# The opening of a decoder layer: norm factors loaded as rows, the first norm in another order, and idle turns on TensorE

## The chip, the core and the metric

The kernel runs on one core of one Trainium2 chip. The metric is the device time of one execution in microseconds (us); lower is better. The core's engines run in parallel, each through a queue of its own: TensorE (PE in the profile; its weight loads are PEld), VectorE (DVE), ScalarE (ACT), GpSimd (POOL) and SyncE (SP), which only issues transfers (DMAs). ACT and POOL issue DMAs too. "SPq" in a view is an instruction of SP's queue. An engine works through its queue in order and waits at an instruction until the semaphores that it names are reached. PE writes to PSUM banks; everything else lives in SBUF (128 partitions).

## What is computed

One layer of a decoder: 16 learned meta tokens are put before 1024 tokens of width 1024, then come a half-step SwiGLU block, a mixer (HGRN2 recurrence beside stick-breaking attention), and a second half-step SwiGLU block, all in float32:

```
def rms_norm(x, gain):
    y = xf * lax.rsqrt(jnp.mean(xf * xf, axis=-1, keepdims=True) + RMS_EPS)
    return (y * gain)

def swiglu(h, w_in, w_out):
    g, u = jnp.split(h @ w_in, 2, axis=-1)
    return (jax.nn.silu(g) * u) @ w_out

h = h + 0.5 * swiglu(rms_norm(h, ffn1_norm), ffn1_w_in, ffn1_w_out)
u = rms_norm(h, mix_norm) @ w_in
...
h = h + o @ w_out
h = h + 0.5 * swiglu(rms_norm(h, ffn2_norm), ffn2_w_in, ffn2_w_out)
```

The part at stake is the first line that uses `ffn1_norm`: the norm of x and the start of its product with `ffn1_w_in`.

## The kernel before

**Precision and tiling.** Each float32 operand is split into a rounded high part (by ACT) and a remainder (by DVE), and each product is three matmuls: high by high, low by high, high by low. A product of 128 output columns with a K of 512 is thus 4 x 3 = 12 matmuls of 128x512, all from one line (L459, `times`). The FFN products use a seven-product scheme (Strassen-Winograd) over 2x2 blocks of x and of the weights; the x operands are called B11, B21, T2, T3, T1, T4 and B22. B11 is the norm's columns 0 to 511 of the first 512 tokens, B21 columns 512 to 1023 of the same tokens.

**The opening.** x comes as eight blocks of 128 tokens by 1024 columns (`ra`, four, then `rb`, four), issued by SP (L820). For each block the squares of a row are summed (`row_sum`: ACT L773 or DVE L770), ACT takes the root of the mean plus epsilon (L778) and DVE the inverse (L779), and DVE scales the block in place (`row_scale`, L785). PE turns 128x128 pieces with the identity into PSUM (`turned`, L794, tile `xps`; one bank per k, that is per 128 columns of x, with a quarter for each block). Then for each k ACT makes the high part times the gain of that k (`first`, L844), and DVE the low part (L845). The gains stand as a column per k, tile `g1`; `ng1` is its negative, needed later.

**Order.** In the opening the queues of PE, ACT, DVE and SP follow the program's order exactly (`manual_schedule`). PE's order is written by hand up to the end; the other engines' queues outside the opening, and POOL's, are put in order by a planner that estimates times and takes what is ready first. The first eight products of weights (four pairs of gate and up, called `quad`) are generators: each call of `next(order[i])` does one step. For a quad the first two steps load half a weight block each (L379 is the load and its rounding), the third multiplies by B11 (12 matmuls into a bank of tag `qa`) and ACT copies the bank (L483), the fourth adds B21. `order[0]` and `order[2]` are the first quad, `order[1]` and `order[3]` the second. After the lines of the change, a loop goes on through the other steps, two loads ahead, with the work on `rb` hung in between: sums, roots, scalings, turns (`turn_b22`, `turn_b12`, `turn_meta`).

**Before, in the program's order:** sum, root and inverse of blocks 0, 1, 2; their scalings; block 3 alone with a scaling in two halves; load step one of both quads; loads of `rb`; turns of all four blocks for k = 0 to 5 (24); operands k = 0 to 3; load step two of the first quad; operands 4 and 5; first quad by B11 (12 matmuls); turns for k = 6 and 7 (8); operands 6 and 7; second quad by B11.

**Gains.** Ten loads bring the small vectors (`column`, L107): each puts one value on each partition, four bytes a piece. The first (`ffn1_norm`) is issued by ACT at the start, the other nine by SP in `setup_rest` (L113), which is called at the end of the opening. The matrix `ones_d` (all 1/1024) is filled at the start and read much later. POOL's first work is to clear `xm` and `actm` (L1816, L1817), then the identity's diagonal (L80, an `affine_select` over ones from DVE), then the cutting of the masks `sd` and `neg_b` (L129 to L142).

Of the kernel before, what the change touches and what calls it, by code (L numbers as in the profile page):

```python
# [11 lines left out]
F32 = mybir.dt.float32  # L12
# [3 lines left out]
AF = mybir.ActivationFunctionType  # L16
ALU = mybir.AluOpType
# [3 lines left out]
P = 128  # L21
D = 1024
KT = D // P
SEQ = 1024
META = 16
T = META + SEQ
D_FF = 2816
EPS = 1e-6
# [21 lines left out]
class Block:  # L50
# [11 lines left out]
            self.tc.tile_pool(name=name, bufs=bufs, **kw)  # L62
        )

    def column(self, src, n, name):
        t = self.const.tile([P, n], F32, name=name)
        self.loads.append((t, src.rearrange("(k p) -> p k", p=P)))
        return t

    def setup(self):  # L70
        nc, a = self.nc, self.a
        self.loads = []
        self.const = c = self.pool("const")
# [5 lines left out]
        nc.vector.memset(self.ident, 1.0)  # L79
        nc.gpsimd.affine_select(  # L80
            out=self.ident, in_=self.ident, pattern=[[-1, P]],
            compare_op=ALU.is_equal, fill=0.0, base=0, channel_multiplier=1,
        )
# [6 lines left out]
        self.g1 = self.column(a["ffn1_norm"][0], KT, "g1")  # L90
        self.gm = self.column(a["mix_norm"][0], KT, "gm")
        self.g2 = self.column(a["ffn2_norm"][0], KT, "g2")
        self.og = self.column(a["hgrn_out_norm"][0], 4, "og")
        self.l0 = self.column(a["hgrn_lb_logits"][0], 4, "l0")
        self.l1 = self.column(a["hgrn_lb_logits"][1], 4, "l1")
        self.qg, self.kg, self.qg8 = (c.tile([P, 1], F32, name=x) for x in ("qg", "kg", "qg8"))
        for h in range(2):
            s = slice(64 * h, 64 * h + 64)
            self.loads.append((self.qg[s], a["sb_q_norm"].rearrange("a d -> d a")))
            self.loads.append((self.kg[s], a["sb_k_norm"].rearrange("a d -> d a")))  # L100
        self.mx, self.lb, self.lbc = (c.tile([P, 4], F32, name=x) for x in ("mx", "lb", "lbc"))
        self.ident_b, self.neg_b = (c.tile([P, P], BF16, name=x) for x in ("ident_b", "neg_b"))
        self.masks = c.tile([P, len(LEVELS), P], U8, name="masks")
        self.ss = c.tile([P, 9, 2], F32, name="ss_x")
        self.ng1 = c.tile([P, KT], F32, name="ng1")
        self.pick = c.tile([P, 2, META], F32, name="pick")
        nc.scalar.dma_start(*self.loads.pop(0))  # L107

    def setup_rest(self):

        nc = self.nc
        for dst, src in self.loads:
# [651 lines left out]
            eng.dma_start(row[:m], x[r0 - META : r0 - META + m, cols])  # L764

    def row_sum(self, row, i, junk, eng):
        nc, m = self.nc, row.shape[0]
        s = self.ss[:m, i, 0:1]
        if eng is nc.vector:
            return eng.scalar_tensor_tensor(  # L770
                junk[1][:m], row, 1.0, row, ALU.mult, ALU.mult, accum_out=s
            )
        return nc.scalar.activation(junk[0][:m], row, AF.Square, accum_out=s)  # L773

    def row_root(self, row, i):
        m = row.shape[0]
        s, r = self.ss[:m, i, 0:1], self.ss[:m, i, 1:2]
        self.nc.scalar.activation(r, s, AF.Sqrt, bias=self.eps[:m], scale=1.0 / D)  # L778
        self.nc.vector.reciprocal(r, r)  # L779

    def row_scale(self, row, i, parts=1):
        m = row.shape[0]
        for j in range(parts):
            t = row[:, D // parts * j : D // parts * (j + 1)]
            self.nc.vector.tensor_scalar_mul(t, t, self.ss[:m, i, 1:2])  # L785

    def turned(self, rows, ks, banks):

        nc = self.nc
        ps = {k: self.pin.tile([P, 512], F32, tag="q" + x, name="xps", bufs=2)  # L790
              for k, x in zip(ks, banks)}
        for i, row in enumerate(rows):
            for k in ks:
                nc.tensor.transpose(  # L794
                    ps[k][:, i * P : (i + 1) * P], row[:, k * P : (k + 1) * P], self.ident
                )
        return ps

    def open_tokens(self, ops, opened, prepare, rows_at, ev, operands):
# [9 lines left out]
        nc, x = self.nc, self.a["x"][0]  # L809
        stt, sub = nc.vector.scalar_tensor_tensor, nc.vector.tensor_sub  # L810
        g = [self.g1[:, k : k + 1] for k in range(KT)]
        rp = self.pool("rows", ctx=rows_at, side="right")
        junk = [rp.tile([P, D], (BF16, U8)[i], name=f"junk{i}") for i in range(2)]
        order = [q for i in range(0, len(opened), 2) for _ in range(2) for q in opened[i : i + 2]]

        def rows_in(r0):
            got = []
            for i in range(4):
                row = rp.tile([P, D], F32, tag="row", name="row", bufs=8)
                nc.sync.dma_start(row, x[r0 + i * P : r0 + i * P + P])  # L820
                got.append(row)
            return got
# [12 lines left out]
        kept = {}  # L835
# [5 lines left out]
        def first(*ks):  # L841
            for k in ks:
                hi, lo = (t[:, k % 4, :] for t in ops[("B11", "B21")[k // 4]])
                nc.scalar.mul(hi, kept[k], g[k])  # L844
# [17 lines left out]
        first(0, 1, 2, 3)  # L862
# [12 lines left out]
        def turn_b22():  # L875
            kept["b22"] = self.turned(rb, range(4, KT), "bbcc")
# [17 lines left out]
        def turn_meta():  # L894
# [18 lines left out]

        def roots():
            for i, row in enumerate(rb + [meta]):
                self.row_root(row, 4 + i)
            for i in range(2):
                self.row_scale(rb[i], 4 + i)

# [866 lines left out]
    def run(self):  # L1786
        nc, tc, a = self.nc, self.tc, self.a
# [11 lines left out]
        n = 512  # L1799
# [8 lines left out]
        with ExitStack() as c0:  # L1808
            with ExitStack() as c1:
# [6 lines left out]
                nc.gpsimd.memset(self.xm, 0.0)  # L1816
                nc.gpsimd.memset(self.actm, 0.0)  # L1817
                with tc.manual_schedule(engines={nc.tensor.engine}), ExitStack() as c2:
                    ev0 = self.pool("ev10", ctx=c2)
                    self.ahead = self.pool("ahead", ctx=c2)  # L1820
# [89 lines left out]
                    first, hooks, steps_ahead = 32, 54, 58  # L1910
# [20 lines left out]
                with tc.manual_schedule(engines={nc.tensor.engine}), ExitStack() as c2:  # L1931
# [48 lines left out]
                    sums, banks = {}, {}  # L1980
# [426 lines left out]
```

## Time and profile before

| | us |
|---|---|
| median of 3 runs | 1965.85 (1964.18 to 1965.95) |
| profiled execution | 1965.29 |
| its span, first to last instruction | 1963.6 |
| PE busy in the span | 1928.3 |
| before PE's first matmul | 11.43 |

How to read it: the page gives busy time by engine, the chain of work that ended last, and groups of instructions by line. `xps<-ident,row` means that the tile `xps` is written from `ident` and `row`; x24 is a count. In the timeline the first number is the start from the span's beginning, the second the length, and square brackets give how long the engine stood idle before and what it waited for. The times of a matmul record overlap with its neighbours, so a group's length over its count is its rate.

### The profile page before, as it was taken

How to read it: one execution, taken by the hardware profiler on the slowest of the kernel's cores; microseconds unless marked ns; L12 is line 12 of the kernel's file. 1: busy time of each engine (PE TensorE's matmuls, PEld its weight loads, DVE VectorE, ACT ScalarE, POOL GpSimd, SP SyncE). 2: the span in 40 equal slices, each digit the busy share in tenths (PEclk: the TensorE clock that was granted, in tenths of full speed). 3: DMA queues.
4: the chain of work that ended last, by engine and by line, in shares of the span. 5: the costliest groups of instructions: out<-in, count | busy, mean ns of one | idle time of the engine just before them, and what ended most of it. 6: DMA issues, size and time to landing. Idle time of an engine off the chain costs nothing.

```text
span 1963.6 us, 30437 instructions
## 1 busy us (share of the span) xinstructions
PE 1928.3 (98%) x10704; PEld 1622.0 (83%) x10704; DVE 1391.6 (71%) x2186; ACT 851.7 (43%) x1711; POOL 449.8 (23%) x626
## 2 busy tenths in 40 slices
PE   7999999999999999999999999999999999999999
PEld 6888888888888888888888978887888888888887
DVE  6977777877678665567777766667567777767774
ACT  6523343334444544356666635433132332344443
POOL 3010100001000003133333332210544545430000
PEclk9999999999999999999999999999999999999999
DMA  6356787757965415865454167655544444469473
GB/s 211 93 160 174 245 278 237 235 208 280 372 226 185 136 47 144 194 175 148 126 143 126 57 249 216 171 204 181 195 117 140 126 137 119 134 236 330 146 232 113
DMA packets 381688, 355.56 MB, mean 181 GB/s; under 512 B 129040, under 2 KB 284560, under 8 KB 381536
## 3 DMA queue, kind: packets, MB, share of 16 engines
q1 hardware_dynamic: 359728, 288.98, 48.2%
q0 software_dynamic: 20768, 64.63, 9.5%
q8 instruction: 85, 1.39, 0.3%
q14 instruction: 67, 0.55, 0.1%
q10 hardware_dynamic: 1040, 0.00, 0.0%
HBM read 237.95 MB, written 115.57 MB: 180 GB/s over the span
## 4 chain that ended last, share of the span: by engine, by line
PE 91%; DVE 4%; DMA 2%; ACT 2%; issue 1%; POOL 0%; SPq 0%; ACTq 0%; DVEq 0%; POOLq 0%
PE o L741 21%; PE qb L459 18%; PE qc L459 12%; PE qa L459 12%; PE proj L258 5%; PE proj L260 5%; PE proj L259 5%; PE flip L1504 2%; PE wo L259 1%; PE wo L260 1%; PE wo L258 1%; PE mq L1010 1%; PE oacc L1579 1%; PE oacc L1581 1%; PE z L1649 1%
## 5 line engine op out<-in xcount | busy, mean ns | idle before, releaser
L459 PE MATMUL qb<-T,wh 128*128 128x512 f32 x1056 | 344.5, 390 | 1.3 <-ACT T L318 0.8
L459 PEld LDWEIGHTS qb<-T,wh 128*128 128x128 f32 x1056 | 198.1, 188 | 46.1 <-issue 2.5
L459 PE MATMUL qa<-B,wh 128*128 128x512 f32 x696 | 226.8, 391 | 0.0
L258 PE MATMUL proj<-xh,wh 128*128 128x512 f32 (+2 forms) x640 | 213.4, 333 | 2.4 <-ACT st L1151 1.3
L741 PE MATMUL o<-t,w 128*128 128x512 f32 x924 | 211.8, 390 | 0.5 <-DVE u L552 0.5
L260 PE MATMUL proj<-xl,wh 128*128 128x512 f32 (+2 forms) x640 | 209.8, 328 | 0.8 <-DVE xl L1973 0.8
L259 PE MATMUL proj<-xh,wl 128*128 128x512 f32 (+2 forms) x640 | 209.7, 328 | 0.0
L741 PE MATMUL o<-parts 128*128 128x512 f32 x924 | 209.6, 389 | 0.0
L459 PE MATMUL qb<-T,wl 128*128 128x512 f32 x528 | 205.4, 389 | 0.0
L741 PEld LDWEIGHTS o<-t,w 128*128 128x128 f32 x924 | 172.8, 188 | 37.3 <-issue 0.8
L741 PEld LDWEIGHTS o<-parts 128*128 128x128 f32 x924 | 173.4, 188 | 36.0
L371 DVE TENSOR_TENSOR wl<-s,wh 128x512 fp32r<-128x512 f32 x160 | 165.8, 1036 | 50.8 <-ACT wh L369 49.8
L369 ACT CAST wh<-s 128x512 fp32r<-128x512 f32 x160 | 99.7, 624 | 188.5 <-PE qb L459 142.3
L459 PEld LDWEIGHTS qa<-B,wh 128*128 128x128 f32 x696 | 130.6, 188 | 27.3 <-DVE B L845 0.3
L369 ACT CAST wh<-raw 128x512 fp32r<-128x512 f32 x120 | 74.6, 622 | 147.3 <-PE qc L459 99.0
L459 PE MATMUL qa<-B,wl 128*128 128x512 f32 x348 | 135.4, 389 | 0.0
L258 PEld LDWEIGHTS proj<-xh,wh 128*128 128x128 f32 x640 | 120.6, 188 | 14.5 <-ACT st L1151 2.0
L260 PEld LDWEIGHTS proj<-xl,wh 128*128 128x128 f32 x640 | 120.5, 188 | 12.1 <-DVE xl L1973 1.2
L259 PEld LDWEIGHTS proj<-xh,wl 128*128 128x128 f32 x640 | 120.5, 188 | 9.9
L459 PE MATMUL qc<-T,wh 128*128 128x512 f32 x352 | 117.0, 394 | 0.0
L459 PE MATMUL qc<-B,wh 128*128 128x512 f32 x352 | 115.1, 390 | 2.0 <-DVE u L552 1.2
L459 PEld LDWEIGHTS qb<-T,wl 128*128 128x128 f32 x528 | 99.1, 188 | 20.4
(398 smaller groups left out, 3853.9 us busy)
## 6 DMA issues: line engine op xcount, KB each, us to landing
raw<-in_ffn_w_in_dram SPq DMA_DIRECT2D x176, 256.0 KB, 3.9
raw<-in_ffn_w_out_dram SPq DMA_DIRECT2D x112, 256.0 KB, 4.4
w2in<-both SPq DMA_DIRECT2D x28, 512.0 KB, 3.4
raw<-in_w_in_dram SPq DMA_DIRECT2D x25, 512.0 KB, 5.1
ks<-kD SPq DMA_DIRECT2D x32, 260.0 KB, 4.7
wout<-both SPq DMA_DIRECT2D x16, 512.0 KB, 3.8
wh<-w2in SPq DMA_DIRECT2D x27, 256.0 KB, 3.5
wl<-w2in SPq DMA_DIRECT2D x27, 256.0 KB, 3.6
```

The source lines that it names most:

```text
L258: nc.tensor.matmul(ps, wh[:, s], xs, start=k == 0, stop=False)
L259: nc.tensor.matmul(ps, wl[:, s], xs, start=False, stop=False)
L260: nc.tensor.matmul(ps, wh[:, s], xl[:, k, c0 : c0 + n], start=False, stop=k == nk - 1)
L369: nc.scalar.copy(hi, src)
L371: self.block_lo = nc.vector.tensor_sub(lo, src, hi.bitcast(F32))
L459: nc.tensor.matmul(ps, a[:, k, :], b[:, k, :], start=start and k == 0 and i == 0, stop=k == 3 and i == 2, skip_group_check=True,)
L741: nc.tensor.matmul(banks[bank][m], y[:, m * P : (m + 1) * P], z, start=start and at == 0 and e == 0, stop=q == nq - 1 and e == 2, skip_gro ...
L1010: nc.tensor.matmul(ps[at : at + 32, at_g, :], self.xm[:, 4 * h + k, :], got[i, h][:, k, :], start=h == 0 and kk == 0, stop=h == 1 and kk = ...
L1504: self.nc.tensor.transpose(ps[:m, j, :], src[:, s0 : s0 + m], self.ident)
L1579: nc.tensor.matmul(o[:, c], vj, w[0], start=j == 0, stop=False, skip_group_check=True)
L1581: nc.tensor.matmul(o[:64, c], vj[:, :64], w[1], start=False, stop=end, skip_group_check=True)
L1649: nc.tensor.matmul(z, q, ks[0][:, s0 : s0 + n], start=True, stop=False)
```

## The change

The ten small vectors are now loaded as 38 rows of 128 values into `ones_d` by POOL, after the identity's select and the two memsets; PE turns the first eight rows (a 128x8 bank `gps`), DVE copies them to `g1` and makes `ng1`. The other 30 are turned later, after step 10 of the loop (`turn_gains`), and `ones_d` gets its 1/1024 in `setup_rest`. POOL now makes the identity before it clears `xm` and `actm`. PE turns the identity into itself 12 times before the factors' turn, 14 times behind it, and 4 times between blocks 0 and 1 (`idle_turns`). Block 3's squares are summed half on ACT, half on DVE, and the second half's mean goes into the root as its bias. Each block is scaled as soon as its inverse is there; of blocks 2 and 3 only columns 0 to 511 are scaled and turned (k = 0 to 3) before operands 0 to 3, the rest after them. The second quad's products by B11 come right behind the first's, ahead of the turns for k = 4 to 7 of the last two blocks; the loads of `rb` come after the first quad's second weight load.

```
     def setup(self):
-        nc.gpsimd.affine_select(
+        self.ident_at = nc.gpsimd.affine_select(
...
-        nc.vector.memset(self.ones_d, 1.0 / D)
...
-        nc.scalar.dma_start(*self.loads.pop(0))
     def setup_rest(self):
-        for dst, src in self.loads:
-            nc.sync.dma_start(dst, src)
+        nc.vector.memset(self.ones_d, 1.0 / D)
...
+    def gain_rows(self):
+        a, at, got = self.a, 0, []
+        for src in (a["ffn1_norm"][0], a["mix_norm"][0], a["ffn2_norm"][0],
+                    a["hgrn_out_norm"][0], a["hgrn_lb_logits"][0], a["hgrn_lb_logits"][1]):
+            src = src.rearrange("(k p) -> k p", p=P)
+            n = src.shape[0]
+            self.loads.append((self.ones_d[at : at + n, :], src))
+            got.append(self.gains[:, at : at + n])
+            at += n
...
+    def row_root(self, row, i, bias=None):
...
+        self.nc.scalar.activation(
+            r, s, AF.Sqrt, bias=self.eps[:m] if bias is None else bias, scale=1.0 / D
+        )
+        return r
...
+    def turn_row(self, ps, row, i, ks):
+        for k in ks:
+            self.nc.tensor.transpose(
+                ps[k][:, i * P : (i + 1) * P], row[:, k * P : (k + 1) * P], self.ident
+            )
...
         ra = rows_in(0)
         self.masks_blank(sd)
-        for i in range(3):
-            self.row_sum(ra[i], i, junk, nc.vector if i == 1 else nc.scalar)
-            self.row_root(ra[i], i)
-        for i in range(3):
-            self.row_scale(ra[i], i)
-        self.row_sum(ra[3], 3, junk, nc.scalar)
-        self.row_root(ra[3], 3)
-        self.row_scale(ra[3], 3, 2)
+        lead = self.pin.tile([P, P], F32, tag="qa", name="lead", bufs=2)
+
+        def idle_turns(count):
+            for _ in range(count):
+                nc.tensor.transpose(lead, self.ident, self.ident)
+
+        idle_turns(12)
+        gps = self.pin.tile([P, KT], F32, tag="qa", name="gps", bufs=2)
+        nc.tensor.transpose(gps, self.ones_d[:KT, :], self.ident[:KT, :KT])
+        idle_turns(14)
+        nc.vector.tensor_copy(self.g1, gps)
+        nc.vector.tensor_scalar_mul(self.ng1, self.g1, -1.0)
+        low, high = slice(0, 512), slice(512, D)
+        invert = nc.vector.reciprocal
+        self.row_sum(ra[0], 0, junk, nc.scalar)
+        r0 = self.row_root(ra[0], 0)
+        self.row_sum(ra[1], 1, junk, nc.vector)
+        invert(r0, r0)
+        self.row_scale(ra[0], 0)
+        r1 = self.row_root(ra[1], 1)
+        self.row_sum(ra[2], 2, junk, nc.scalar)
+        invert(r1, r1)
+        self.row_scale(ra[1], 1)
+        r2 = self.row_root(ra[2], 2)
+        self.row_sum(ra[3][:, low], 3, junk, nc.scalar)
+        self.row_sum(ra[3][:, high], 8, junk, nc.vector)
+        rest = self.ss[:, 8, 1:2]
+        nc.vector.tensor_scalar(
+            rest, self.ss[:, 8, 0:1], 1.0 / D, EPS, ALU.mult, ALU.add
+        )
+        invert(r2, r2)
+        self.row_scale(ra[2], 2, low)
+        r3 = self.row_root(ra[3], 3, rest)
+        invert(r3, r3)
+        self.row_scale(ra[3], 3, low)
         next(order[0])
-        next(order[1])
-        rb = rows_in(512)
-        meta = rp.tile([META, D], F32, name="meta")
-        kept.update(self.turned(ra, range(6), "bbccdd"))
+        kept.update(self.xps(range(6), "bbccdd"))
+        for i in range(2):
+            self.turn_row(kept, ra[i], i, range(6))
+            idle_turns(4 * (i == 0))
+        for i in (2, 3):
+            self.turn_row(kept, ra[i], i, range(4))
         first(0, 1, 2, 3)
+        next(order[1])
+        for i in (2, 3):
+            self.row_scale(ra[i], i, high)
         nc.vector.tensor_scalar_mul(b11[0], kept[0], g[0])
         spare(1)
         next(order[2])
+        rb = rows_in(512)
+        meta = rp.tile([META, D], F32, name="meta")
         nc.sync.dma_start(meta, self.a["meta_tokens"])
-        first(4, 5)
-        self.row_sum(rb[0], 4, junk, nc.vector)
         next(order[0])
         next(order[1])
+        next(order[3])
+        for i in (2, 3):
+            self.turn_row(kept, ra[i], i, (4, 5))
+        first(4, 5)
         kept.update(self.turned(ra, (6, 7), "bb"))
         first(6, 7)
-        next(order[3])
+        self.row_sum(rb[0], 4, junk, nc.vector)
...
+        def turn_gains():
+            ps = self.pin.tile([P, 38], F32, tag="qd", name="gps", bufs=2)
+            nc.tensor.transpose(ps, self.ones_d[:38, :], self.ident[:38, :38])
+            nc.vector.tensor_copy(self.gains[:, KT:], ps[:, KT:])
...
-        after = {6: turn_b22, 7: turn_b12, 8: turn_meta}
+        after = {6: turn_b22, 7: turn_b12, 8: turn_meta, 10: turn_gains}
...
-                nc.gpsimd.memset(self.xm, 0.0)
-                nc.gpsimd.memset(self.actm, 0.0)
+                with tc.issue_after(self.ident_at):
+                    nc.gpsimd.memset(self.xm, 0.0)
+                    nc.gpsimd.memset(self.actm, 0.0)
+                    for dst, src in self.loads:
+                        nc.gpsimd.dma_start(dst, src)
...
-                    nc.vector.tensor_scalar_mul(self.ng1, self.g1, -1.0)
```

`issue_after(x)` puts the instructions of its block behind x in the same engine's queue, with no wait for x to end.

More of the change, by code (lines that the diff above doesn't have):

```diff
@@ L63, in pool @@
         )
[L65 to L68, printed above, removed]
+    def gain_rows(self):
[7 more added lines that the diff above has]
+            at += n
+        for src in (a["sb_q_norm"], a["sb_k_norm"]):
+            for h in range(2):
+                self.loads.append((self.ones_d[at : at + 1, 64 * h : 64 * h + 64], src))
+            got.append(self.gains[:, at : at + 1])
+            at += 1
+        return got
     def setup(self):
@@ L72, in setup @@
         self.loads = []
-        self.const = c = self.pool("const")
+        c = self.pool("const")
         c.tile([P, 208], F32, name="base")
@@ L79, in setup @@
         nc.vector.memset(self.ident, 1.0)
-        nc.gpsimd.affine_select(
+        self.ident_at = nc.gpsimd.affine_select(
             out=self.ident, in_=self.ident, pattern=[[-1, P]],
             compare_op=ALU.is_equal, fill=0.0, base=0, channel_multiplier=1,
-        )
+        ).ins
         self.ones_d = c.tile([P, P], F32, name="ones_d")
-        nc.vector.memset(self.ones_d, 1.0 / D)
         self.eps = c.tile([P, 1], F32, name="eps")
@@ L88, in setup @@
         nc.scalar.activation(c.tile([P, 1], F32, name="root"), self.eps, AF.Sqrt)
[L90 to L100, printed above, removed]
+        self.gains = c.tile([P, 38], F32, name="gains")
+        self.g1, self.gm, self.g2, self.og, self.l0, self.l1, self.qg, self.kg = self.gain_rows()
+        self.qg8 = c.tile([P, 1], F32, name="qg8")
         self.mx, self.lb, self.lbc = (c.tile([P, 4], F32, name=x) for x in ("mx", "lb", "lbc"))
@@ L766, in row_sum @@
     def row_sum(self, row, i, junk, eng):
-        nc, m = self.nc, row.shape[0]
+        nc, (m, n) = self.nc, row.shape
         s = self.ss[:m, i, 0:1]
@@ L770, in row_sum, with row_scale, xps @@
             return eng.scalar_tensor_tensor(
-                junk[1][:m], row, 1.0, row, ALU.mult, ALU.mult, accum_out=s
+                junk[1][:m, :n], row, 1.0, row, ALU.mult, ALU.mult, accum_out=s
             )
-        return nc.scalar.activation(junk[0][:m], row, AF.Square, accum_out=s)
-    def row_root(self, row, i):
+        return nc.scalar.activation(junk[0][:m, :n], row, AF.Square, accum_out=s)
+    def row_root(self, row, i, bias=None):
         m = row.shape[0]
         s, r = self.ss[:m, i, 0:1], self.ss[:m, i, 1:2]
[L778 to L785, printed above, removed]
+        self.nc.scalar.activation(
+            r, s, AF.Sqrt, bias=self.eps[:m] if bias is None else bias, scale=1.0 / D
+        )
+        return r
+    def row_scale(self, row, i, cols=slice(0, D)):
+        t = row[:, cols]
+        self.nc.vector.tensor_scalar_mul(t, t, self.ss[: row.shape[0], i, 1:2])
+    def xps(self, ks, banks):
+        return {k: self.pin.tile([P, 512], F32, tag="q" + x, name="xps", bufs=2)
+                for k, x in zip(ks, banks)}
+    def turn_row(self, ps, row, i, ks):
[3 more added lines that the diff above has]
+            )
     def turned(self, rows, ks, banks):
-        nc = self.nc
-        ps = {k: self.pin.tile([P, 512], F32, tag="q" + x, name="xps", bufs=2)
-              for k, x in zip(ks, banks)}
+        ps = self.xps(ks, banks)
         for i, row in enumerate(rows):
[L793 to L796, printed above, removed]
+            self.turn_row(ps, row, i, ks)
         return ps
@@ L858, in open_tokens @@
+        invert(r2, r2)
[3 more added lines that the diff above has]
+        self.row_scale(ra[3], 3, low)
+        next(order[0])
+        kept.update(self.xps(range(6), "bbccdd"))
[4 more added lines that the diff above has]
+            self.turn_row(kept, ra[i], i, range(4))
+        first(0, 1, 2, 3)
         next(order[1])
-        rb = rows_in(512)
@@ L860, in open_tokens @@
-        meta = rp.tile([META, D], F32, name="meta")
-        kept.update(self.turned(ra, range(6), "bbccdd"))
-        first(0, 1, 2, 3)
+        for i in (2, 3):
+            self.row_scale(ra[i], i, high)
         nc.vector.tensor_scalar_mul(b11[0], kept[0], g[0])
@@ L915, in roots @@
             for i, row in enumerate(rb + [meta]):
-                self.row_root(row, 4 + i)
+                r = self.row_root(row, 4 + i)
+                invert(r, r)
             for i in range(2):
```

## The prediction

> **What bounds the kernel now.** I read the page first: the span, the busy shares and the chain of waits by engine.
>
> ```profile
> span 1963.6 us, 30437 instructions
> ...
> PE 1928.3 (98%) x10704; PEld 1622.0 (83%) x10704; DVE 1391.6 (71%) x2186; ACT 851.7 (43%) x1711; POOL 449.8 (23%) x626
> ...
> PE 91%; DVE 4%; DMA 2%; ACT 2%; issue 1%; POOL 0%; SPq 0%; ACTq 0%; DVEq 0%; POOLq 0%
> ```
>
> TensorE (PE) is the bound, so the change can only be worth the idle or slow PE time that it removes. Next, PE's busy time by stretch of the span (length, busy time, instructions, then the other columns):
>
> ```profile
> 0.00:11.42 11.42, 0.00 (x0) 1.00 0.81 282
> ...
> 20.65:80.00 59.35, 59.34 (x283) 1.00 0.36 95
> ```
>
> PE does nothing for 11.42 us, and from 20.65 to 80 it is never idle. So whatever the opening gains by the point where PE goes on without a pause is carried on, and nothing after it in this stretch repays a delay. Third, the chain of waits over the first 80 us (start, length, what):
>
> ```profile
> 1.25 5.97 DMA row<-in_x_dram
> ...
> 7.24 1.35 DVE junk L770 x2
> ...
> 8.61 0.29 ACT ss_x L778
> 8.91 1.05 ACT junk L773 x2
> ...
> 10.40 0.89 DVE row L785
> ...
> 11.43 5.36 PE xps L794 x24
> 16.78 3.09 PE qa L459 x12
> 19.87 1.02 PE xps L794 x8
> 20.90 16.35 PE qa L459 x72
> ```
>
> The second row block of x lands at 7.22, its squares are summed on VectorE (DVE), ScalarE (ACT) takes roots in order, all four blocks' factors come before the first scaling, and PE turns at 11.43. The 24 turns take 0.21 us each (5.06 from 11.43 to the first product at 16.49); the later ones are faster (a window of the turns alone, then all turns of the opening, ns shortest, median and longest):
>
> ```profile
> 19.71:20.64 0.93, 0.93 (x8) 0.73 (x7) 0.41 (x2) 0.72 (x2) 1.00 1.15 345
> ```
>
> ```profile
> L794 PE MATMUL xps<-ident,row x32: 270/421/448, 11.4 to 20.6; 128*128 128x128 f32 x32
> ```
>
> 0.93/8 is 0.116 us per turn, and the shortest record is 270 ns against a median of 421: the first turns run at about half rate. The granted clock in the windows reads 1.00 there, so the half rate is seen in the durations only.
>
> **The loads.** ACT issued the first norm's factors at the start as a column. The rows are the DMA issues (KB, us to landing), four windows of one microsecond (last columns DMA share and GB/s), and ACT's first sum in the timeline.
>
> ```profile
> g<-in_ffn_norm_dram ACTq DMA_DIRECT2D x1, 4.0 KB, 5.3
> ```
>
> ```profile
> 3.00:4.00 1.00, 0.00 (x0) 0.00 (x0) 0.00 (x0) 0.00 (x0) 1.00 (x3) 1.00 0.86 175
> 4.00:5.00 1.00, 0.00 (x0) 0.00 (x0) 0.00 (x0) 0.59 (x1) 1.00 (x2) 1.00 0.67 153
> 5.00:6.00 1.00, 0.00 (x0) 0.00 (x0) 0.00 (x0) 0.86 (x3) 1.00 (x4) 1.00 0.98 373
> ...
> 7.00:8.00 1.00, 0.00 (x0) 0.00 (x0) 0.76 (x1) 0.00 (x0) 1.00 (x3) 1.00 1.00 410
> ```
>
> ```profile
> 4.41 1.06 ACT L773 ACTIVATE junk<-row 128x1024 bf16<-128x1024 f32 x1 [1.62 <-DMA row<-in_x_dram]
> ```
>
> While the column came, the engines were 0.67 to 0.98 busy and moved 153 to 373 GB/s instead of 410. The shortfall is 235 + 257 + 37 = 529 KB, 1.3 us at 410 GB/s. Without it the second block lands at 7.22 - 1.3 = 5.95. Bounds: 7.22 if the dip is not the column's; 5.65 if blocks follow the first (4.4) at 512 KB per 1.25 us. I take 5.95. Block one stays at 4.4.
>
> **The new factor load.** It goes by POOL, behind the identity's select and two memsets.
>
> ```profile
> 0.81 0.31 POOL L1816 MEMSET xm<- 128x256 f32 x1 [0.29 <-POOLq L2393]
> ...
> 0.91 0.17 DVE L79 MEMSET ident<- 128x128 f32 x1 [0.91 <-PEq L2393]
> ...
> 1.05 0.69 POOL L1817 MEMSET actm<- 128x704 f32 x1
> ...
> 1.79 0.29 POOL L80 TENSOR_SCALAR_AFFINE_SELECT ident<-ident 128x128 f32<-128x128 f32 x1
> ...
> 13.25 1.08 POOL L142 TENSOR_SCALAR_AFFINE_SELECT sd<-sd 128x64 f32<-128x64 f32 x2
> ...
> 31.16 0.72 POOL L556 DMA_DIRECT2D act10B<-sg  x1 [16.83 <-DVE sg L549]
> ...
> 40.49 0.62 DVE L937 CAST masks<-sd 128x896 uint8<-128x896 f32 x1
> ```
>
> ```profile
> act11B<-sg POOLq DMA_DIRECT2D x1, 256.0 KB, 2.6
> ...
> act10B<-sg POOLq DMA_DIRECT2D x1, 256.0 KB, 4.0
> ```
>
> DVE's memset ends at 1.08; the select follows to 1.45, PE's idle turns start at 1.5, and the memsets (0.81 to 1.79, 0.98 us) end at 2.4. POOL's own transfers land 2.6 us (quiet) or 4.0 us (busy) after issue: L = 5.0 to 6.4. The load is eight rows of 512 bytes, so I take the lower, L = 5.0. Nine more loads and the mask cutting follow on POOL. At 0.72 us per issue the masks move some 7 us later, from 14.3 to about 21; DVE reads them at 40.49, so that costs nothing unless this cover shrinks by 19 us.
>
> **What queues behind it.** DVE runs in order here: behind its copy of the turned factors stand every row sum, inverse and scaling. After L come one turn (0.42), the copy (0.17), the negated copy and their hand-overs (0.3): DVE is free at L + 0.9 = 5.9. The row sum of block two starts at s = 6.0, set by the load of x.
>
> ```profile
> 7.24 1.33 DVE L770 SCALAR_TENSOR_TENSOR junk<-row 128x1024 uint8<-128x1024 f32 x1 [0.49 <-DMA row<-in_x_dram]
> ...
> 10.40 2.20 DVE L785 TENSOR_SCALAR row<-row,ss_x 128x1024 f32<-128x1024 f32 x3
> 12.52 0.15 DVE L779 RECIPROCAL ss_x<-ss_x 128x1 f32<-128x1 f32 x1
> 12.71 0.88 DVE L785 TENSOR_SCALAR row<-row,ss_x 128x512 f32<-128x512 f32 x2
> ...
> 15.75 2.43 ACT L844 ACTIVATE B<-xps,g 128x512 fp32r<-128x512 f32 x4 [3.08 <-PE xps L794]
> ```
>
> DVE from s: row sum 1.35; four inverses with hand-over 0.2 each (12.52 to 12.71); two full scalings 2.20/3 = 0.73 each; half a row sum 0.7; one tiny operation 0.1; two half scalings 0.44 each. Sum 1.35 + 0.8 + 1.46 + 0.7 + 0.1 + 0.88 = 5.3, so the last half block is ready at 11.3. ACT's roots fit: block three's squares (1.05, plus 0.3 for the root) and half of block four's end some 0.3 us before DVE asks. One warm turn (0.27) and hand-overs later, ACT makes the first operand at 11.7. Before it was 15.75. **Lead there: 4.05 us.** PE is ready for that: 14 idle turns after the factors at 0.21 end at 8.45, block one is scaled at 8.3, and the other turns fit between the scalings if the clock is up.
>
> **What the new order gives back.** Count from the first operand (0). Before (15.75): first product at 16.49, 12 products to the turns at 19.71 (3.22, paced by ACT and DVE), eight turns 0.94, 12 products 2.73 (16.35/72 x 12), 12 more 2.73: that is 0.74 + 3.22 + 0.94 + 2.73 + 2.73 = 10.36. After: 12 paced (0.74 + 3.22), then the second 12 at once (2.73, plus 0.1 for its weights, which DVE splits after the four operands), ending at 6.79; then 12 turns (1.4) to 8.18. ACT first copies the bank of those products, then makes operand five:
>
> ```profile
> 23.68 0.59 ACT L483 COPY p<-qa 128x512 f32<-128x512 f32 x1 [1.08 <-PE qa L459]
> 24.16 0.62 ACT L369 CAST wh<-raw 128x512 fp32r<-128x512 f32 x1
> ...
> 31.84 0.59 ACT L483 COPY both<-qa 128x512 f32<-128x512 f32 x1 [0.76 <-PE qa L459]
> ```
>
> By 23.68 against PE's 23.38 (20.65 + 2.73) the copy starts 0.3 later, at 7.09, and holds ACT 0.48 (its next starts at 24.16): operand five at 7.57, its product at 8.31, and these 12 are paced again, 3.22: 11.53. So 11.53 - 10.36 = **1.17 us go back**. ACT does not fall behind afterwards: from 23.68 to 31.84 it worked 8.16 - 0.76 = 7.4 us, four operands more make 9.83, and it is ready at 7.09 + 9.83 = 16.92 where PE's bank is done at 17.3.
>
> **Sum:** 4.05 - 1.17 = 2.9 us off. The idle turns and the one later turn of 38 rows (0.12) lie in PE's empty time or are under 0.2. The nine column loads that leave SP's queue gain nothing, since PE did not wait from 20.65 to 80. On SP the second four blocks and the meta rows move behind one more weight load: 256 KB, 0.6 us at 410 GB/s, covered by the 1.3 us that the stream gains; DVE's first sum over them now comes after all eight operand pairs, later than before against PE, so without that cover it still would not wait. The profiled execution took 1965.29 (1963.6 and 1.69 around it): 1962.4. The median of the runs is 0.56 higher, which gives 1962.95; I predict 1962.7, between the two.
>
> **A rule against it.** The first 12 products took 0.26 us each (3.09/12) directly behind 5 us that held turns alone, near the steady 0.227; turns raised the rate here. The Trainium skill, "TensorE: Matmul & The Clock Gate", Part 4 (PE-mode transpose), says that the full clock does not engage for transposes, since they don't count as busy in the same way. By that rule the idle turns could not warm PE and the sum would be rival 2's, about 1965; this trace disagrees, with 0.26 us where a half-rate product would be near 0.4.
>
> **Rivals.**
> 1. *Better than the sum.* Block two lands at 5.65 and DVE is free by then (0.3), the second pacing costs nothing (3.22 + 0.13 wait against 2.73: 0.6), and the planner, which orders the queues of ACT, DVE, POOL and SP outside the opening by estimated times, spares a few of PE's later waits: 2.9 + 0.9 = 3.8 and more, 1961.5 down to 1959.5. It needs nearly all of these at once. Chance 0.30.
> 2. *The clock isn't up.* PE rests from 4.0, when 12 idle turns end, to 5.1, and the turns must fill an unknown window; by the rows it took 5 us of unbroken turns. If cold, block four's first turn is issued at 8.45 + 20 x 0.21 = 12.65 and done at 13.07 instead of 11.65: 1.4 us lost, and up to 1.6 more if the first 12 products run at 0.41 (an estimate, 0.227 x 0.21/0.116) instead of 0.27: 1964 to 1965.7. Against it: from 5.1 on PE is busy without a gap. Chance 0.10.
> 3. *The factors come late: slower.* DVE and PE both stand in order behind them. Every microsecond of L past 5.1 costs one; the gain is gone at L = 8.0, that is 5.6 us from issue to landing. At L = 10 the time is 1967.3. For it: the same 4 KB took 5.3 us by ACT in the same place. Against: that was a column of 4-byte pieces, and POOL's rows show 2.6 and 4.0. Chance 0.06.
> 4. *The planner orders the rest otherwise.* Ten loads move from SP and ACT to POOL, and the planner may place others differently behind them. PE's waits after the opening are many short ones; the largest group has this row:
>
> ```profile
> PE flip L1504 <- DVE wu L1628: 3.0, 7, 0.7
> ```
>
> A handful of new ones at 0.7 us cost 3 to 8: 1966 to 1970. Nothing in this trace decides it. Chance 0.08.
>
> **How the numbers follow.** The forecast has 0.46: 1961.9 to 1964.5. About 0.2% (3.9 us) is what a measurement here can tell from no change. Faster by more: rival 1, 0.30, plus 0.02 of the forecast's edge, 0.32. Slower by more: most of rival 4 (0.06) and of rival 3 what needs L over 12 (0.02), 0.08. Within: the rest, 0.60. The range, 1960.5 to 1966.3, leaves out the far end of rival 1 and most of 3 and 4.
>
> **What would show it.** Right: the factors' turn near 5.1 and DVE's first row sum near 6.0; the last half scaling ending near 11.3; turns of blocks three and four at 0.12 apart; the first product near 12.4; PE without a pause from about 20 us; 1.2 us lost between the first and third dozen products. Wrong: POOL's load landing after 6, turns at 0.21 when block three comes, the second block still at 7.2, or a changed sum of PE's idle time after 80 us.

## The result, and the profile after

| | before | after |
|---|---|---|
| median of 6 runs each | 1964.18 (1962.96 to 1965.95) | 1977.88 (1976.43 to 1980.93) |
| profiled execution | 1965.29 | 1978.02 |
| its span | 1963.6 | 1976.3 |
| PE busy in the span | 1928.3 | 1947.7 |

After over before is 1.0071, with a 95% interval of 1.006 to 1.0082: slower by 13.7 us, where the prediction's sum had 2.9 us off. One line of the diff above is wrong: it shows ACT's load of the first norm's factors as taken away, but in the kernel that ran the line stands. ACT issues that load, now as eight rows; only the other nine go by POOL.

The opening first: ACT, PE and DVE in the timeline of after (start, length, what, idle before).

```profile
0.81 0.58 ACTq L109 DMA_DIRECT2D ones_d<-in_ffn_norm_dram  x1
...
7.47 1.06 ACT L774 ACTIVATE junk<-row 128x1024 bf16<-128x1024 f32 x1 [0.24 <-DMA row<-in_x_dram]
...
11.63 2.43 ACT L850 ACTIVATE B<-xps,gains 128x512 fp32r<-128x512 f32 x4 [0.71 <-PE xps L794]
```

```profile
1.49 2.82 PE L859 MATMUL lead<-ident 128*128 128x128 f32 x12 [1.49 <-POOL ident L91]
4.24 0.27 PE L863 MATMUL gps<-ident,ones_d 8*128 8x8 f32 x1
4.45 1.90 PE L859 MATMUL lead<-ident 128*128 128x128 f32 x14
...
12.37 0.50 PE L460 MATMUL qa<-B,wh 128*128 128x512 f32 x1 [0.45 <-ACT B L850]
```

```profile
5.67 1.22 DVE L771 SCALAR_TENSOR_TENSOR junk<-row 128x1024 uint8<-128x1024 f32 x1 [0.74 <-DMA row<-in_x_dram]
...
9.08 0.73 DVE L771 SCALAR_TENSOR_TENSOR junk<-row 128x512 uint8<-128x512 f32 x1 [0.45 <-DMA row<-in_x_dram]
...
10.71 0.49 DVE L786 TENSOR_SCALAR row<-row,ss_x 128x512 f32<-128x512 f32 x1
```

Block two's sum starts at 5.67 instead of 7.24, the last half scaling ends at 11.20, the first operand starts at 11.63 and the first product at 12.37 instead of 16.49. So the opening gains what it was to gain. The loss comes later. First a window of PE in after (length, busy time, instructions, granted clock; then DMA share and GB/s), then the chain of waits in after and the chain in before, in the two FFNs:

```profile
80.00:200.00 120.00, 120.00 (x723) 1.00 0.59 161
```

```profile
36.47 2.81 PE qa L460 x12
...
83.90 5.60 PE qb L460 x24
89.50 5.60 PE qc L460 x24
...
1372.04 5.44 PE qb L460 x24
...
1415.56 2.81 PE qa L460 x12
```

```profile
39.43 2.74 PE qa L459 x12
...
84.99 5.44 PE qb L459 x24
90.43 5.44 PE qc L459 x24
...
1361.89 5.44 PE qb L459 x24
...
1405.41 2.72 PE qa L459 x12
```

PE is busy for the whole 120 us from 80 to 200, at a granted clock of 1.00, as it was in before, and still falls behind. The same 24 products take 5.60 us instead of 5.44: 233.3 ns each instead of 226.7. In the first FFN this holds for `qa`, `qb` and `qc`. In the second it holds for `qa` alone (12 in 2.81 against 2.72); 24 of `qb` keep 5.44 in the same stretch, and so do the 24 of `qc` behind them. The page agrees: PE's idle time went down by 6.7 us (35.3 to 28.6, span less busy), and its busy time went up by 19.4, of which the 32 added turns are 5.8 by their rows.

How many products are affected, by the lines of after (duration of one record, shortest, median and longest, then first and last start):

```profile
L460 PE MATMUL qb<-T,wh x1056: 387/392/505, 64.4 to 1760.0; 128*128 128x512 f32 x176
...
L460 PE MATMUL qa<-B,wh x696: 388/396/502, 12.4 to 1751.8; 128*128 128x512 f32 x174
...
```

The eight such groups, of which these are the two largest, count 3684, so 1842 in each FFN, and 522 of them are `qa` (696 + 348 over two). In the first FFN 1842 by 6.7 ns (0.16/24) and in the second 522 by 7.5 ns (0.09/12) give 12.3 + 3.9 = 16.2 us. That is 2.5 us more than the 13.7 measured, which leaves room for what the opening gains; how much of that gain reaches the end is seen in the experiments.

**The theory.** Nothing in the change names these products, but it moves their operands. SBUF's tiles are laid out from two ends, here called its left and its right side. Before, eight small vectors each had a tile on the left side, and each took 32 bytes of every partition, 256 together. The one tile `gains` holds 38 values in 152 bytes and takes 160. So every tile that is placed after it on the left side, the split weights `wh` and `wl` among them, starts 96 bytes lower in the compiled program (`wh` at 53152 instead of 53248), while the tiles on the right side stay (B11 at 188416). The weights are the stationary operand of a product, the one that PE loads first; the x operand moves past it. In the first FFN the moving operands of all three groups lie on the right; in the second only `qa`'s (B11, B21) do, while `qb` and `qc` take both operands from the left. The theory: the pitch of a product, the time from its start to the next one's, depends on the distance between the addresses of its stationary and its moving operand.

### The profile page after: what moved, and what is told of

Its sections match the earlier page's. It is cut to its first block, busy times and chain, and to the rows that moved or that the text cites. A ratio compares the mean times of both kernels' runs of the same rounds, so it can differ in the third digit from the quotient of the medians.

```text
span 1976.3 us, 30518 instructions
## 1 busy us (share of the span) xinstructions
PE 1947.7 (99%) x10736; PEld 1624.8 (82%) x10736; DVE 1387.2 (70%) x2192; ACT 850.9 (43%) x1711; POOL 455.3 (23%) x635
## 4 chain that ended last, share of the span: by engine, by line
PE 89%; DVE 4%; DMA 4%; ACT 1%; issue 1%; SPq 1%; POOL 0%; DVEq 0%; ACTq 0%; POOLq 0%
PE o L742 21%; PE qb L460 18%; PE qa L460 12%; PE qc L460 12%; PE proj L259 5%; PE proj L261 5%; PE proj L260 5%; DMA raw<-in_ffn_w_in_dram 2%; PE flip L1552 2%; PE wo L260 1%; PE wo L261 1%; PE wo L259 1%; PE oacc L1627 1%; PE oacc L1629 1%; PE mq L1058 1%
## 5 line engine op out<-in xcount | busy, mean ns | idle before, releaser
L460 PE MATMUL qa<-B,wh 128*128 128x512 f32 x696 | 231.7, 397 | 0.6 <-ACT B L850 0.4
L372 DVE TENSOR_TENSOR wl<-s,wh 128x512 fp32r<-128x512 f32 x160 | 161.1, 1007 | 55.1 <-ACT wh L370 54.0
```

What stands on the lines that cost most here:

```text
L372: self.block_lo = nc.vector.tensor_sub(lo, src, hi.bitcast(F32))
L460: nc.tensor.matmul(ps, a[:, k, :], b[:, k, :], start=start and k == 0 and i == 0, stop=k == 3 and i == 2, skip_group_check=True,)
```

## The experiments

### The distance between the operands

Three kernels tell the theory from its rivals, which were that the new order or the new loads slow PE, that the early idle turns do, or that one absolute address is bad. The first takes the changed kernel and puts 96 unused bytes behind `gains`:

```
         self.gains = c.tile([P, 38], F32, name="gains")
+        c.tile([P, 24], F32, name="pad")
```

> The changed kernel with 24 unused columns (96 bytes) behind the new tile of factors, so that every tile from qg8 on has the address that it had in the kernel before. Address theory: the products' pitch in the first FFN goes back from 232 to 227 ns, its 469 us back to some 456, and the whole takes about 1961 us (1964.2 less the 3 us that the opening gained by the turns of the last blocks, 39.43 against 36.47). Rival, the planner's other order of queues and loads: nothing changes, 1977 to 1979. Rival, TensorE runs slower after its early idle turns: nothing changes either, 1977 to 1979.

The second takes the kernel before and moves its left side, with nothing else changed (`base` is a tile that nothing reads):

```
-        c.tile([P, 208], F32, name="base")
+        c.tile([P, 184], F32, name="base")
```

> The kernel before with its unused tile base cut from 208 to 184 columns, so that all that follows on the left lies 96 bytes lower, as in the changed kernel; nothing else is changed. Address theory: 1848 products of the first FFN at 6.3 ns more (11.6 us) and 528 of the second at 7.5 (4.0 us): 1979 to 1980. Both rivals: 1964 to 1965, pitch 227.

The third takes the changed kernel and lowers the right side by the same 96 bytes (`edge` is unused too):

```
-        self.pool("edge", side="right").tile([P, 504], F32, name="edge")
+        self.pool("edge", side="right").tile([P, 528], F32, name="edge")
```

> The changed kernel with the unused tile edge grown from 504 to 528 columns, so that the tiles on the right side (the FFN's x operands) lie 96 bytes lower too. If the pitch depends on where the stationary operand lies relative to the moving one: 227 ns in both FFNs, 1961 us. If it depends on each operand's own address: 232 ns in the first FFN and also in its second half and in the second FFN, 1978 us or more. Both rivals: 1977 to 1979.

The chain of waits of the three, in that order:

```profile
44.14 5.71 PE qa L461 x24
49.84 0.18 PE gps L949
...
63.83 5.45 PE qb L461 x24
69.30 0.69 DVE u L493
70.00 0.60 DVE s L393
70.59 1.20 DVE b L1006 x2
71.80 0.61 DVE wl L373
...
72.45 2.81 PE qb L461 x11
75.27 2.72 PE qc L461 x12
...
82.81 5.44 PE qb L461 x24
```

```profile
85.78 5.60 PE qb L459 x24
...
1344.65 16.82 PE qa L459 x72
```

```profile
83.21 5.44 PE qb L460 x24
```

| kernel | median us | over before (95%) |
|---|---|---|
| after, 96 bytes put back | 1962.94 | 0.9996 (0.9987 to 1.0004) |
| before, left side 96 bytes lower | 1979.02 | 1.0077 (1.0063 to 1.0091) |
| after, right side lowered as well | 1964.16 | 1.0 (0.9991 to 1.0009) |

One number in the kernel before costs as much as the whole change (15.3 us over the before of its set); 96 unused bytes in the changed kernel take the loss away. The third shows that it is the distance and no absolute place: with both sides lower, the left side's addresses are those of the changed kernel and the right side's are new, and the pitch is 226.7 again. In the second kernel the second FFN's `qa` has 72 products in 16.82 us, 233.6 each, as in the changed one. The two kernels that got their pitch back came out 2 and 3 us above the 1961 us that was expected of them: the opening's gain does not show in their medians (0.8 us under before and 0.4 above, with intervals on both sides of 1).

One more rival is that other engines' or DMA traffic to the moved tiles slows PE's reads. The trace of after speaks against it: of 1515 products of the first FFN that follow one of their kind, 32 ran while no operation of DVE, ACT or POOL and no DMA packet was under way, and they are 233.4 ns apart, where all 1515 average 233.3. And before itself holds 12 products at another distance: in its compiled program the two addresses lie a whole multiple of 512 bytes apart for 3684 of these products, and 64 bytes off that for the 12 that read the tiles `w0h` and `w0l`, at the start of the second FFN. These 12, with both operands on the right, are 229 ns apart.

A fourth kernel checks the sum from the other side: the changed kernel with `base` 232 in place of 208, so that the constants lie 96 bytes higher than in the changed kernel and all tiles behind `gains` lie where they did before.

> The changed kernel with the unused tile base grown from 208 to 232 columns instead of a pad behind the factors: from qg8 on the addresses are those of the kernel before, the identity, ones_d and the factors lie 96 bytes higher. Address theory: pitch 227 in both FFNs and the time of the padded kernel, 1961 to 1963.5; the opening ends 2.5 to 3.2 us earlier than before. Rivals (queues, early idle turns): 1977 to 1979.

It took 1963.42 us, 0.9996 (0.9988 to 1.0005), as with the pad.

Three more move the left side of the kernel before by other distances: `base` 192 (64 bytes lower), 200 (32) and 176 (128).

> The kernel before with base cut to 192 columns: the left side 64 bytes lower. Address theory, if a step of 64 bytes between the two operands is harmless: pitch 227 and 1964 to 1965. If only a whole 128 bytes (or more) is: pitch above 230 in the first FFN and 1972 to 1985. Both rivals: 1964 to 1965.

> The kernel before with base cut to 200 columns: the left side 32 bytes lower. 64 bytes lower gave a pitch of 229 and 96 bytes lower one of 232. If the pitch grows with the distance to the next multiple of 128: 229 or more, as far from it as 96 is, up to 232 and 1979. If it grows with the bytes by which the left side lies lower: 228 and 1966 to 1968. If only the step modulo 64 counts, as with 96 bytes: 232 and 1979.

> The kernel before with its left side of SBUF 128 bytes lower, nothing else. Theory (what counts is the distance between the two operands' addresses, taken modulo 128 bytes): 227 ns per product in both FFNs and 1963 to 1966 us, as before. Rival (a longer period, or any move at all from the places of before): 229 ns or more and 1970 to 1979 us.

Their chains of waits, a row of the first FFN and one of the second each, 64 bytes, 32 and 128 in turn:

```profile
85.03 5.49 PE qb L459 x24
...
1411.00 2.76 PE qa L459 x12
```

```profile
85.93 5.60 PE qb L459 x24
...
1413.95 2.80 PE qa L459 x12
```

```profile
85.79 5.58 PE qb L459 x24
...
1415.76 2.79 PE qa L459 x12
```

| left side lower by | 24 products of the first FFN, us | median us | over before (95%) |
|---|---|---|---|
| 0 | 5.44 | 1963.7 to 1964.9 | 1 |
| 32 bytes | 5.60 | 1977.51 | 1.0068 (1.0048 to 1.0087) |
| 64 bytes | 5.49 | 1970.18 | 1.0026 (1.0011 to 1.004) |
| 96 bytes | 5.60 | 1979.02 | 1.0077 (1.0063 to 1.0091) |
| 128 bytes | 5.58 | 1975.56 | 1.0054 (1.0036 to 1.0073) |

The 64-byte run met neither of its two forecasts: 228.8 ns lies between them, and so does the time. Its pitch is that of the 12 products above. The 128-byte run refutes the finer form of the theory, a period of 128 bytes. No distance but that of before gave the full rate; since before has whole multiples of 512 bytes, a period of 256 or 512 fits all rows, and no run tried it. What in the memory sets the pattern stays open.

### Idle turns

The padded kernel without its 30 idle turns (`idle_turns` loops zero times), twice, the second time beside the padded kernel with them on the same chip:

> The changed kernel with the 96 unused bytes of the first experiment, and without the 30 idle turns (the one turn of the factors stays). If the idle turns raise the rate before x comes: the 20 turns before the first operand take 0.21 instead of 0.12 us each, the first operand comes some 0.4 us later than 11.6, and the first dozen products are up to 1.6 us longer; the opening ends 0.4 to 2.0 us later than with them, the whole takes 0.4 to 2.0 us more than the padded kernel. If turns don't raise the rate, or x is what the opening waits for anyway: the same as the padded kernel within 0.3.

> The change with the 96 bytes put back and without the 30 idle turns, a second time, beside the version with them on the same chip. If the idle turns cost time later on: 1961 to 1961.6, and 1.5 to 2.5 us under the version with them. If the earlier difference was luck between runs: within 0.7 us of it.

> The change with the 96 bytes put back and all idle turns, a second time: 1962.5 to 1963.5 us as the first time, if the spread between chips and runs is small; under 1962 if its first result was bad luck.

The first without turns took 1961.3 us, 0.9986 (0.9977 to 0.9994), where the same or 0.4 to 2.0 us more than with turns was expected; the kernel with `base` 232, which has the turns, ran beside it and took 2.1 more. In the second set it took 1962.17, 0.9984 (0.9976 to 0.9993), the one with turns 1964.21, 0.9997 (0.9988 to 1.0006). Both absolute forecasts were 0.6 to 0.7 us low, and the kernel before was 0.9 longer on that chip than beside the first set (1964.87 against 1964.0); the difference of 2.0 is in the 1.5 to 2.5 that were expected if the turns cost time. In the opening they do not. PE in the timeline without turns (first set), then in the padded kernel with them (second set):

```profile
2.88 0.24 PE L864 MATMUL gps<-ident,ones_d 8*128 8x8 f32 x1 [2.88 <-DMA ones_d<-in_ffn_norm_dram]
8.00 4.56 PE L795 MATMUL xps<-ident,row 128*128 128x128 f32 x20 [4.88 <-DVE row L787]
...
34.31 2.34 PE L795 MATMUL xps<-ident,row 128*128 128x128 f32 x16
```

```profile
33.84 2.34 PE L795 MATMUL xps<-ident,row 128*128 128x128 f32 x16
```

These sixteen are the first turns of `rb`. In before they start at 37.09, here at 34.31 and at 33.84: 2.78 and 3.25 us earlier. The other two profiles say the same: 34.25 without turns in the second set, 33.92 with them in the first padded run. So the turns earn some 0.4 us there (with `base` 232 the sixteen start at 34.34, but there DVE waited for the last block of x until 9.54, where it had begun at 8.69 with the pad), and yet the kernels with them come out 2.1 and 2.0 us longer. The profiled executions do not show where: with turns the second set's span was 1958.6 us, without them 1961.4, against the medians. That the kernel without turns is the fastest of all that ran, and faster than before, is measured twice. The intervals of the two kernels overlap, so the size of the turns' cost is less sure than its sign; why they cost time is open.

### Rows or column

The padded kernel, with the first norm's factors loaded as a column of 4-byte pieces again, straight into `gains`. PE turns a piece of the identity in place of the factors, and DVE clears the first eight rows of `ones_d`, which nothing fills now, just ahead of the later turn of the other 30 (the cut shows the load alone):

```
-            self.loads.append((self.ones_d[at : at + n, :], src))
+            if at == 0:
+                self.loads.append((self.gains[:, :n], src.rearrange("k p -> p k")))
+            else:
+                self.loads.append((self.ones_d[at : at + n, :], src))
```

> The padded kernel in which the first norm's factors come as a column of 4-byte pieces by ACT, as before, straight into their tile; the factors' turn and copy are left out (a turn of identity rows stands in their place). If the column costs the stream of x 1.3 us: block two is summed at 7.2 instead of 5.7 and the opening ends 1.0 to 1.6 us later than in the padded kernel. If the dip in the transfers was not the column's: the sum starts within 0.4 us of 5.7.

It took 1969.02 us, 1.0024 (1.0014 to 1.0034): 6.1 us more than the padded kernel, 5.6 more than the one with `base` 232, which ran beside it. Windows of PE with rows, then with the column (the last two figures are DMA share and GB/s), then the later turn in PE's timeline with the column:

```profile
4.00:5.00 1.00, 1.00 (x6) 1.00 0.97 369
```

```profile
4.00:5.00 1.00, 1.00 (x8) 1.00 0.75 146
...
14.70:18.20 3.50, 3.50 (x9) 0.51 1.10 340
18.20:21.00 2.80, 2.80 (x14) 1.00 1.15 345
...
55.50:59.10 3.60, 3.60 (x10) 0.53 0.26 72
```

```profile
55.00 0.22 PE L952 MATMUL gps<-ident,ones_d 38*128 38x38 f32 x1 [1.90 <-issue]
```

The dip in the stream of x is the column's, as the prediction read it: block two's sum starts at 7.14 with the column and at 5.80 with rows, 1.34 us apart against 1.3 predicted. The 6.1 us hold more than that. PE stood idle for 3.10 us before block one was scaled, and from 14.7 the granted clock was 0.51 for 3.5 us: 9 products where 14 take 2.80. At the first turns of `rb` this kernel is 3.33 us behind the padded one (37.25 against 33.92). The rest is the experiment's own doing and not the column's: the clearing of `ones_d` stands in DVE's queue behind other work until 54.74, PE waits 1.90 us for it at the turn above, and a second window of low clock, 0.53 from 55.5 to 59.1, follows that pause. By the rows at 89.10 and 82.81 the two kernels are 6.29 us apart, and the medians say the same. So the column's own cost is some 3.3 us, an estimate from the rows at the first turns of `rb`, and about half of what the medians show.

### Rows alone

The padded kernel with factors as rows, but the opening in the order of before and no idle turns:

> One part alone: factors as rows turned by TensorE, the opening in the order of before, no idle turns, 96 bytes put back. Theory (two shares, the rows give what the x stream gains, the order the rest): the sum over block two starts near 5.8 where it was 7.24, the first turns near 10.0 where they were 11.43, and TensorE is 1.3 to 1.6 us ahead of before at 40 us, against 2.8 to 3.1 for rows and order together; time 1962.5 to 1964. Rival one (the rows give all of it): 2.8 or more ahead at 40 us. Rival two (the order gives all of it): under 0.5 us ahead.

Its DVE and PE in the timeline:

```profile
6.28 0.16 DVE L864 RECIPROCAL ss_x<-ss_x 128x1 f32<-128x1 f32 x1 [2.79 <-ACT ss_x L780]
6.36 1.21 DVE L772 SCALAR_TENSOR_TENSOR junk<-row 128x1024 uint8<-128x1024 f32 x1
...
9.39 3.15 DVE L787 TENSOR_SCALAR row<-row,ss_x 128x1024 f32<-128x1024 f32 x3
```

```profile
36.38 2.34 PE L795 MATMUL xps<-ident,row 128*128 128x128 f32 x16
```

It took 1964.07 us, 0.9993 (0.9985 to 1.0002). Block two's sum starts at 6.36, not near 5.8, and PE's first turn at 10.67, not near 10.0. PE is 0.71 us ahead of before at the first turns of `rb` (36.38 against 37.09), less than the 1.3 to 1.6 of the theory and more than the rival's 0.5. In the old order block two's sum stands behind the first inverse, which waits for ACT's root until 6.28, so of the 1.44 us by which the padded kernel's sum is earlier (7.24 to 5.80) it has 0.88; and the three scalings took 3.15 us, against 2.20 in before, for a reason that this run does not show. By the first turns of `rb` (37.09 in before; in this set 36.38, 34.25 without idle turns and 33.84 with them) the gain at that point divides into 0.7 for the rows, 2.1 for the order and 0.4 for the turns.

## Why the prediction was wrong

- **The step that failed is the sum.** "2.9 us off" was set against the whole time of before, as though nothing outside the opening changed. The term left out is the tiles' addresses: 96 bytes less on the left side, 6.7 ns more per product in the first FFN and 7.5 for `qa` in the second, 16.2 us. The opening's share of the sum came true, as the points below show. No rival held the loss. Rival 4 had one after the opening, but by waits; the sign named for it, a changed sum of PE's idle time after 80 us, cannot show a PE that stays busy and does less. With the addresses put back, 0.8 us of the 2.9 are left by the medians, and that is not clear of no change.
- **The new factor load** was put on POOL with L = 5.0. It stayed on ACT, and with rows had landed by 2.9 at the latest: without idle turns ahead of it the factors' turn ran then. So rival 3 had no ground. DVE was free at 4.92 where 5.9 was predicted, and it was x that set the sum's start either way.
- **The loads of x.** Block two came at 5.67, as in the lower bound (5.65) and 0.3 earlier than taken. The wait went to blocks three and four: ACT waited for the one until 7.47, DVE for the other until 9.08. The work was predicted to be paced by DVE alone; the two differences cancel, which is luck, and the last half scaling ended at 11.20 (predicted 11.3).
- **The lead** at the first operand was 15.75 - 11.63 = 4.12 us (predicted 4.05), and 39.43 - 36.47 = 2.96 us were left at the first product behind those turns of `rb` (predicted 2.9). Of the 1.16 given back, some 0.4 is the slower pitch (58 products by 6.7 ns); with the pad the lead fell from 4.06 to 3.17, that is by 0.89 against the predicted 1.17. So the close agreement of 2.96 with 2.9 is in part luck.
- **"Nothing after it in this stretch repays a delay"** was only partly right. With the pad the lead is 2.18 us by the rows at 84.99 and 82.81, where it was 3.17. The chain of waits of the padded kernel, shown above, has a piece that the chain of before does not have, through DVE's `u`, `s`, `b` and `wl` at 69.30: PE comes to the next half of its weights before DVE has split it. From 63.83 to 75.27 is 11.44 us, against 10.90 for 48 products in before, 0.54 lost. The stretch ahead of it took 19.69 us where 84 products took 19.27: 0.42, of which the later turn of the other factors (`gps`) is 0.18. The wait is not the price of the lead: the kernel with rows alone, only 0.71 us ahead, has it too, and its lead is gone by 85 us (in PE's timeline `qb` starts at 85.06, against 84.83 in before). What differs is the order in which the planner put DVE's queue, here in before and then with rows alone:

```profile
72.93 0.68 DVE L957 TENSOR_TENSOR b<-b,t 128x512 f32<-128x512 f32 x1
73.53 0.69 DVE L371 TENSOR_TENSOR wl<-s,wh 128x512 fp32r<-128x512 f32 x1
```

```profile
72.90 1.29 DVE L978 TENSOR_TENSOR b<-b,t 128x512 f32<-128x512 f32 x2
74.11 0.69 DVE L373 TENSOR_TENSOR wl<-s,wh 128x512 fp32r<-128x512 f32 x1
```

  In before, `s` comes ahead of `u` and one `b` ahead of `wl`; in the others `s` comes behind `u`, and two `b` stand ahead of `wl`. That is rival 4's mechanism, at half a microsecond.
- **The clock.** Rival 2, which the prediction held to be unlikely, did not come true. Twelve idle turns took 2.82 us, 0.235 each, and the next 14 took 1.90, 0.136 each, so the rate rose while PE did nothing but turns. The trace's record of the granted clock agrees: it begins, at full clock, 4.8 us into the span of after, 16.9 in before, and 13.7 in the first run without idle turns. The Trainium skill, "TensorE: Matmul & The Clock Gate", Part 4, by which transposes do not engage the full clock, does not hold here by these rows.

## What to carry to other kernels

An edit that adds, merges or drops a persistent tile moves every tile behind it, so hold the later addresses fixed with a pad, or compare the pitch of untouched matmuls (24 in the chain of waits, before and after) before the edit itself is judged. A busy engine at full granted clock can still be slow: read the time that a fixed number of equal products takes, and not only busy time. A gain at the start is kept only if the queues behind it serve it; here another order of DVE's queue and a later turn made 3.2 us into 2.2 by 85 us, and in the medians of the padded kernel the rest was hardly to be told from no change. And read the trace of an experiment before its total: the run with the column held a wait that the edit itself had made.

## What was not expected of the hardware

- The pitch of a 128x512 float32 matmul depended on the distance between its stationary and its moving operand in SBUF: 226.7 ns at that of before, 228.8 with 64 bytes less, 232.5 with 128, 233.3 with 32 or 96. Products whose two operands moved together did not change.
- After 3.1 us without work for PE, in the run with the column, the granted clock fell to 0.51 for 3.5 us although PE had been busy again for most of 5 us; after a pause of 1.90 us in the same run it fell again, to 0.53 for 3.6 us. In the runs without idle turns PE rested 4.88 us, and its next 20 turns took 0.228 us each.
